# Cross-attention keys: 512-byte pieces and turns on VectorE instead of transposes on TensorE

## The chip, the cores and the metric

The kernel runs on one core of a Trainium2 chip. The metric is the device time of one execution in microseconds (us). Engines are called as in the profile: PE is TensorE, DVE VectorE, ACT ScalarE, POOL GpSimd and SP SyncE.

## What is computed

One inference step of a hybrid decoder layer, for a prompt group (1 x 256 tokens) and a sample group (8 x 4 tokens) that share the weights: a Mamba-2 branch and a gated linear attention branch, merged by gates, then cross-attention into 256 memory tokens, then a convolutional feed-forward network. All data are 32-bit floats. The change is in the cross-attention (4 heads of 512 channels, model width 2048):

```python
def _cross_attend(hn, mem_k, mem_v, w_cq, w_co):
    Bsz, L, _ = hn.shape
    q = (hn @ w_cq).reshape(Bsz, L, CROSS_HEADS, CROSS_HEAD_DIM).astype(jnp.float32)
    s = jnp.einsum('blhd,bmhd->bhlm', q, mem_k.astype(jnp.float32)) * (CROSS_HEAD_DIM ** -0.5)
    pr = jax.nn.softmax(s, axis=-1)
    o = jnp.einsum('bhlm,bmhd->blhd', pr, mem_v.astype(jnp.float32)).astype(hn.dtype)
    return o.reshape(Bsz, L, D_MODEL) @ w_co
```

The prompt attends to keys and values that the kernel has computed and stored earlier; each of the 8 samples has its own keys and values in a cache (8 x 256 x 4 x 512).

## The kernel before, in words

**Tokens and weights.** Activations lie with channels on the 128 partitions and all T = 288 tokens (256 of the prompt, 32 of the samples) along the free dimension. A weight matrix streams through in blocks: `wload` (L108) issues the DMA on SP's queue into one of three `raw` buffers of 512 KB, and `wsplit` (L100) divides a block into a high half, cast by ACT (L103), and a low half, subtracted by DVE (L105); five buffers of each let this run ahead of PE. `proj_w` (L132) then makes three matmuls of 288 columns for every 128 x 128 weight block: high by high, high by low, low by high (L147, L148, L151). It covers 256 output columns at a time in two PSUM banks; `acc_tiles` (L61) alternates between two pairs of banks, so one pair is emptied while the other fills. A "row block" below is 128 input rows against four column blocks, 12 matmuls.

**Order of the work.** `weave` (L172) runs a main generator, the projection of the next head, and after each of its steps the due share of a background generator, the attention of this head. Within that order a scheduler may move instructions of an engine whose dependences allow it, except those held by `keep_in_program_order`. Each engine executes its own queue in order. DMAs issued by POOL stand in POOL's queue, weights in SP's.

**Around the cross-attention.** `gate_b` (L1262) ends the gating, `w_mix_out` is projected (L1303 to L1309) with residuals loaded and stored by POOL in pieces of two tiles, and then the stage begins:

- `q_proj(hd)` (L1359) projects the queries of one head in two passes of 256 columns, each over all 16 row blocks. For each 128 columns DVE scales the sum from PSUM into the one `qs` buffer (L1370), ACT and DVE split it into `qh` and `ql`, and `diag` (L194) spreads the sample columns into `xqm`, which has zeros outside each sample's own columns.
- `attend(hd)` (L1380) takes a key tile of one sample as [128 tokens, 2, 512 channels] (`mem_rows`, L1375, one DMA of 512 KB on POOL's queue, at most four loaded ahead in five buffers), transposes it in eight 128 x 128 blocks through PE (`transpose_half`, L1347, matmuls of L1353 into PSUM), and copies the result out in two halves, one by DVE and one by ACT (L1410), into `kT`. After each four samples `scores` (L1398) multiplies all sample queries with these keys (L1402). The prompt's keys go the same way but are split in two halves (L1421), and the prompt scores are made from them (L1431 to L1433). Softmax (L1338), transposes of the probabilities (L1446, L1455), products with the values of samples (L1464) and prompt (L1474 to L1476), and a fold of the sample rows (L1484) follow. The values of four samples lie in the large buffer `vq` (L1412), those of the others come through the same five buffers as the keys.
- `run(q_proj(0))` stands alone (L1496); then four rounds weave `attend(hd)` with `q_proj(hd + 1)`, in the last round with the first 12 steps of the output projection `w_co` (L1497 to L1499). One such round is called a head's turn below.

Of the kernel before, what the change touches and what calls it, by code (L numbers as in the profile page):

```python
# [20 lines left out]
NB = 8  # L21
# [21 lines left out]
def hybrid_step(ctx: ExitStack, tc: tile.TileContext, I: dict, O: list):  # L43
# [56 lines left out]
    def wsplit(raw):  # L100

        hi = wp.tile(list(raw.shape), F32R, tag="whi", bufs=WB, name="whi")
        S.copy(hi, raw)  # L103
        lo = wp.tile(list(raw.shape), F32R, tag="wlo", bufs=WB, name="wlo")
        V.tensor_tensor(lo, raw, hi, ALU.subtract)  # L105
        return hi, lo
# [1146 lines left out]
    mx = halves(bigr2, "mx")  # L1253
    pc_cm = pool("pc")
# [48 lines left out]
    for j2 in range(KT // 2):  # L1303
# [4 lines left out]
        if j2 + 3 < KT // 2:  # L1308
            load_x(j2 + 3)  # L1309
    rst.append(acc)  # L1310
# [6 lines left out]
    def x4(name):  # L1317
        return px.tile([P, 2, 512], F32, tag="x4", bufs=5, name=name)

    def k4(name):  # L1320
        return px.tile([P, 4, 256], F32, tag="k4", bufs=5, name=name)

# [3 lines left out]
    def q2(name):  # L1326
        return px.tile([P, 2, 256], F32R, tag="q2", bufs=6, name=name)
# [19 lines left out]
    def transpose_half(kv, d2):  # L1347

        a = mm_tile()
        for d in range(2):  # L1350
            for m in range(2):
                dd = 2 * d2 + d
                TR(a[:, d * 256 + m * P:d * 256 + (m + 1) * P], kv[:, m, dd * P:(dd + 1) * P], ident)  # L1353
        return a.rearrange("p (d m) -> p d m", m=256)

# [3 lines left out]
    def q_proj(hd):  # L1359
        qp = []  # L1360
        qps.append(qp)
        for j2 in range(2):
            def cons(j, a, j2=j2):
                if not rc:
                    rc.append(rstd_of())
                if j == 0:
                    qp.append((q2("qh"), q2("ql")))
                d = 2 * j2 + j
                qs = px.tile([P, T], F32, tag="qs", bufs=1, name="qs")
                V.tensor_tensor(qs, a, rc[0], ALU.mult)  # L1370
                split(qp[j2][0][:, j, :], qp[j2][1][:, j, :], qs[:, 0:SEQ])
                diag(xqm[hd % 2][:, d], qs[:, SEQ:T])
            yield from proj(I["w_cq"], 512 * hd + 256 * j2, 256, hn, KT, cons)

    def mem_rows(src, name):  # L1375
        t = x4(name)
        G.dma_start(out=t, in_=src.rearrange("(m p) d -> p m d", p=P))
        return t

    def attend(hd):  # L1380


        xq = xqm[hd % 2]
        loads = [(I["cache_mem_k"][b, :, hd, :], "kc") for b in range(NB)]
        loads += [(o_pmk[0, :, hd, :], "kp"), (o_pmv[0, :, hd, :], "vp")]
        loads += [(I["cache_mem_v"][b, :, hd, :], "vc") for b in range(4, NB)]
        got = []
        vq = big.tile([P, 4, 2, 512], F32, tag="bigf", bufs=1, name="vq")

        def rows():  # L1390
            while loads and len(got) < 4:
                got.append(mem_rows(*loads.pop(0)))
            return got.pop(0)

        ssc = la_tile()
        kT = []

        def scores(q):  # L1398
            for d in range(4):
                for j in (3, 2, 1, 0):  # L1400
                    b = 4 * q + j
                    MM(ssc[NS * j:NS * j + NS, 0:256], xq[:, d, b, :], kT[b][:, d, :], start=(q == 0 and d == 0),  # L1402
                       stop=(q == 1 and d == 3))

        for b in range(NB):
            kc = rows()
            kT.append(k4("kT"))
            for d2 in range(2):
                a = transpose_half(kc, d2)
                (S.copy if d2 else V.tensor_copy)(kT[b][:, 2 * d2:2 * d2 + 2, :], a)  # L1410
            if b < 4:
                G.dma_start(out=vq[:, b], in_=I["cache_mem_v"][b, :, hd, :].rearrange("(m p) d -> p m d", p=P))  # L1412
            yield
            if b == 4:
                scores(0)
                yield
        kp = rows()
        kh, kl = r4("kTh"), r4("kTl")
        for d2 in range(2):
            a = transpose_half(kp, d2)  # L1420
            split(kh[:, 2 * d2:2 * d2 + 2, :], kl[:, 2 * d2:2 * d2 + 2, :], a)  # L1421
        yield
        scores(1)
        yield
        prs = []
        for l in range(2):
# [7 lines left out]
            if l == 0:  # L1434
                pr = k4("prs")[:, 0, :]
# [5 lines left out]
        vp = rows()  # L1441
        vh, vl = v2("vph"), v2("vpl")
        split(vh, vl, vp)
        a = mm_tile()
# [15 lines left out]
        vcs = [vq[:, b] for b in range(4)] + [rows() for _ in range(4)]  # L1460
        for q in (1, 0):
            for m in range(2):
                for j in (3, 2, 1, 0):
                    mm = MM(osa[NS * j:NS * j + NS, :], pms[:, m, 4 * q + j, :], vcs[4 * q + j][:, m, :],  # L1464
                            start=(q == 1 and m == 0), stop=(q == 0 and m == 1))
                    if q == 1 and m == 0 and j == 3:
                        tc.keep_in_program_order(mm)
        yield
        yield
        for d in range(4):  # L1470
# [6 lines left out]
            split(*(x[:, 0:SEQ] for x in co(4 * hd + d)), a[:, 0:SEQ])  # L1477
            yield
        os_ = k4("os").rearrange("p d m -> p (d m)")[:, 0:512]
# [8 lines left out]


# [6 lines left out]
    run(q_proj(0))  # L1496
    for hd in range(4):  # L1497
        main = q_proj(hd + 1) if hd < 3 else chain(steps(wo[0], 6), steps(wo[1], 6))
        weave(main, attend(hd), 16 if hd < 3 else 12, 21)  # L1499
    px_cm.__exit__(None, None, None)  # L1500

# [238 lines left out]
```

## Time and profile before

| What | Value |
|---|---|
| Time, median of 3 runs | 2555.09 us (2553.22 to 2556.65) |
| Profiled execution: span | 2555.0 us |
| PE busy | 2536.1 us, 99% |
| DVE, ACT, POOL busy | 1733.3, 1353.1, 400.0 us |
| Moved by DMA | 521.96 MB, mean 204 GB/s |
| The stage: first query matmul to last fold | about 1416 to 1631 us of the span |

The profile page gives no time of the profiled execution other than its span, from the first to the last instruction. Busy time counts an engine's instructions, overlapped or not, so PE at 99% says that matmuls follow each other closely, not that PE is at its peak. The chain of waits is followed back from the last instruction of a window to whatever released each one; its shares add up to the window. In the table of stages the columns are busy microseconds of PE, PE's weight loads, DVE, ACT and POOL with the number of instructions, then the granted PE clock (1.00 is full), the share of time for which the 16 DMA engines held packets, and the rate in GB/s.

### The profile page before, as it was taken

To read this page: it belongs to the slowest core of one execution; us is meant where nothing else is said; L and a number is where in the kernel's file an instruction comes from. 1 tells how busy PE (TensorE), PEld (TensorE's weight loads), DVE (VectorE), ACT (ScalarE), POOL (GpSimd) and SP (SyncE) were. 2 spreads that over 40 slices of the span, in tenths; PEclk is the share of its full clock that TensorE was granted. 3 is DMA by queue.
4 is the path that set the end of the run, shared out by engine and by line. 5 is a ranking of instruction groups with operands and counts; after the bars stand their busy time and mean duration, and the time that the engine had idled before them with its cause. 6 is when DMAs were issued, how large, how long until landed. Compare 5 with 4: busy or idle time off the path is not lost.

```text
span 2555.0 us, 50480 instructions
## 1 busy us (share of the span) xinstructions
PE 2536.1 (99%) x18966; PEld 2440.0 (95%) x18966; DVE 1733.3 (68%) x3672; ACT 1353.1 (53%) x2712; POOL 400.0 (16%) x741
## 2 busy tenths in 40 slices
PE   9999999999999999999999999999999999999998
PEld 8889999999999999999999989999999999999998
DVE  6656777796767666766556555567777677675765
ACT  7656547645364555444545544456545455454545
POOL 3002234241201000010000122412010101020010
PEclk9999999999999999999999999999999999999999
DMA  8676587776868585777666778755555555555553
GB/s 267 216 223 200 170 243 212 225 208 193 233 194 287 171 259 166 242 234 246 184 207 212 250 260 304 221 172 171 166 175 166 175 166 175 167 171 171 169 172 128
DMA packets 442277, 521.96 MB, mean 204 GB/s; under 512 B 27132, under 2 KB 390492, under 8 KB 441968
## 3 DMA queue, kind: packets, MB, share of 16 engines
q1 hardware_dynamic: 407728, 422.34, 53.7%
q0 software_dynamic: 34272, 96.38, 12.2%
q8 instruction: 149, 2.44, 0.4%
q14 instruction: 96, 0.79, 0.1%
q10 hardware_dynamic: 32, 0.01, 0.0%
HBM read 473.13 MB, written 45.48 MB: 203 GB/s over the span
## 4 chain that ended last, share of the span: by engine, by line
PE 96%; DVE 1%; DMA 1%; issue 0%; ACT 0%; POOL 0%; DVEq 0%; ACTq 0%
PE acc L148 27%; PE acc L147 27%; PE acc L151 26%; PE acc L315 2%; PE acc L316 2%; PE acc L319 2%; PE mm L1353 1%; PE la L1402 1%; PE mm L1147 1%; PE la L1138 1%; PE la L1464 1%; PE mm L1111 1%; DMA raw<-in_w_ssd_out_dram 0%; DMA raw<-in_w_in_dram 0%; PE la L864 0%
## 5 line engine op out<-in xcount | busy, mean ns | idle before, releaser
L105 DVE TENSOR_TENSOR wlo<-raw,whi 128x512 fp32r<-128x512 f32 x1464 | 998.4, 687 | 666.3 <-ACT whi L103 636.1
L103 ACT CAST whi<-raw 128x512 fp32r<-128x512 f32 x1464 | 897.9, 618 | 1023.3 <-PE acc L148 807.9
L147 PE MATMUL acc<-xn,whi 128*128 128x288 f32 (+1 forms) x1936 | 550.7, 300 | 0.0
L148 PE MATMUL acc<-xn,whi 128*128 128x288 f32 (+1 forms) x1936 | 542.4, 296 | 0.0
L151 PE MATMUL acc<-xn,wlo 128*128 128x288 f32 (+1 forms) x1936 | 414.5, 295 | 0.0
L148 PE MATMUL acc<-hf,whi 128*128 128x288 f32 x1408 | 393.3, 295 | 0.0
L147 PE MATMUL acc<-hf,whi 128*128 128x288 f32 x1408 | 389.0, 292 | 0.0
L147 PEld LDWEIGHTS acc<-xn,whi 128*128 128x128 f32 (+1 forms) x1936 | 364.9, 188 | 9.8 <-issue 8.1
L148 PEld LDWEIGHTS acc<-xn,whi 128*128 128x128 f32 (+1 forms) x1936 | 365.1, 189 | 6.8 <-issue 4.8
L151 PEld LDWEIGHTS acc<-xn,wlo 128*128 128x128 f32 (+1 forms) x1936 | 310.8, 188 | 1.3 <-issue 1.1
L151 PE MATMUL acc<-hf,wlo 128*128 128x288 f32 x1408 | 294.4, 290 | 0.0
L148 PEld LDWEIGHTS acc<-hf,whi 128*128 128x128 f32 x1408 | 264.5, 188 | 0.1
L147 PEld LDWEIGHTS acc<-hf,whi 128*128 128x128 f32 x1408 | 264.0, 188 | 0.1
L151 PEld LDWEIGHTS acc<-hf,wlo 128*128 128x128 f32 x1408 | 226.3, 188 | 0.0
L148 PE MATMUL acc<-pr,whi 128*128 128x288 f32 x704 | 196.5, 295 | 0.0
L147 PE MATMUL acc<-pr,whi 128*128 128x288 f32 x704 | 195.0, 293 | 0.0
L151 PE MATMUL acc<-pr,wlo 128*128 128x288 f32 x704 | 147.4, 290 | 0.0
L147 PE MATMUL acc<-un,whi 128*128 128x288 f32 x512 | 145.7, 300 | 1.6 <-DVE ma L955 1.6
L148 PE MATMUL acc<-un,whi 128*128 128x288 f32 x512 | 143.0, 294 | 0.0
L1564 POOL COPY fsp<-fst 128x16 f32<-128x16 f32 x88 | 36.3, 415 | 650.2 <-DVE av L1576 426.5
L148 PEld LDWEIGHTS acc<-pr,whi 128*128 128x128 f32 x704 | 132.3, 188 | 0.0
L147 PEld LDWEIGHTS acc<-pr,whi 128*128 128x128 f32 x704 | 132.0, 188 | 0.0
(508 smaller groups left out, 4347.7 us busy)
## 6 DMA issues: line engine op xcount, KB each, us to landing
raw<-in_w_in_dram SPq DMA_DIRECT2D x240, 512.0 KB
raw<-in_w_up_dram SPq DMA_DIRECT2D x176, 512.0 KB
raw<-in_w_down_dram SPq DMA_DIRECT2D x88, 512.0 KB
raw<-in_w_cv_dram SPq DMA_DIRECT2D x32, 512.0 KB
raw<-in_w_ssd_out_dram SPq DMA_DIRECT2D x32, 512.0 KB
sin<-in_state_gla_dram POOLq DMA_DIRECT2D x32, 512.0 KB, 5.9
out_dram<-sin SPq DMA_DIRECT2D x32, 512.0 KB
raw<-in_w_gla_out_dram SPq DMA_DIRECT2D x32, 512.0 KB
```

The source lines that it names most:

```text
L103: S.copy(hi, raw)
L105: V.tensor_tensor(lo, raw, hi, ALU.subtract)
L147: MM(a, hi[:, k, cs], xh, start=(k0 + s0 + k == 0), stop=False)
L148: MM(a, hi[:, k, cs], xl, start=False, stop=False)
L151: MM(a, lo[:, k, cs], xh, start=False, stop=(k0 + s0 + k == nk - 1))
L315: MM(accs[m], mn_hi[:, kk, ms_], hi[:, 0, :], start=(kk == 0), stop=False)
L316: MM(accs[m], mn_lo[:, kk, ms_], hi[:, 0, :], start=False, stop=False)
L319: MM(accs[m], mn_hi[:, kk, ms_], lo[:, 0, :], start=False, stop=(kk == KT - 1))
L1111: MM(a, kt[:, i, k * P:(k + 1) * P], vt[i], start=True, stop=True)
L1138: MM(osa[NS * j:NS * j + NS, :], qdm[:, k, b, :], sins[b][:, k, :], start=False, stop=(q == 1 and k == 0))
L1147: MM(a, kb[:, k * P:(k + 1) * P], vst, start=True, stop=True)
L1564: G.tensor_copy(sp[:, :, 0:2], st.rearrange("p (b k) -> p b k", k=2))
```

## The change

Keys are loaded so that DVE can finish the transposition. A key tile becomes [128, 1024]: four DMAs, one for each 128 channels i, each writing 32 partitions. Partition 32 i + m holds, for t = 0 to 7, the 128 channels (512 bytes) of token 32 t + m. DVE's transpose works on blocks of 32 x 32; two of them in place (512 columns each) leave on partition 32 i + x channel 128 i + 32 j + x, for j = 0 to 3, of each token. So the channel tile j that a score matmul contracts over consists of four runs of 32 channels, and the query columns are put in the same order when the query weights are split.

For this `q_proj` handles all 512 columns of a head in one pass: its weight loads take rows of 2 KB for two row blocks, all four accumulator banks are held, and the scale factor is computed at the fifth row block. `transpose_half`, the copies to `kT` and the tiles `x4` and `k4` go. A pool `pk`, opened before the gating ends, has ten tiles for keys and values; the first head's keys are loaded one by one during `gate_b`, its prompt keys and values and four samples' values during the projection of `w_mix_out`. Later heads' loads are issued in `attend` at places where their buffers have just been read. The first head's keys are turned beside `q_proj(0)`, four keys of a later head beside the last products of the head before it.

```diff
-    def wsplit(raw):
-
-        hi = wp.tile(list(raw.shape), F32R, tag="whi", bufs=WB, name="whi")
-        S.copy(hi, raw)
-        lo = wp.tile(list(raw.shape), F32R, tag="wlo", bufs=WB, name="wlo")
-        V.tensor_tensor(lo, raw, hi, ALU.subtract)
+    def wsplit(raw, order=None):
+
+        view = (lambda t: t.rearrange(order)) if order else (lambda t: t)
+        shape = list(raw.shape)
+        if order:
+            shape = [shape[0], shape[2], shape[1], shape[3]]
+        hi = wp.tile(shape, F32R, tag="whi", bufs=WB, name="whi")
+        S.copy(view(hi), raw)
+        lo = wp.tile(shape, F32R, tag="wlo", bufs=WB, name="wlo")
+        V.tensor_tensor(view(lo), raw, view(hi), ALU.subtract)
         return hi, lo
...
+    def mem_load(hd, kind, b=0):
+
+        t = pk.tile([P, 1024], F32, tag="k4", bufs=10, name={"k": "kc", "kp": "kp", "vp": "vp", "v": "vc"}[kind])
+        if kind in ("k", "kp"):
+            src = I["cache_mem_k"][b, :, hd, :] if kind == "k" else o_pmk[0, :, hd, :]
+            for i in range(4):
+                tc.keep_in_program_order(G.dma_start(
+                    out=t[32 * i:32 * i + 32].rearrange("p (t x) -> p t x", x=P),
+                    in_=src[:, i * P:(i + 1) * P].rearrange("(t m) x -> m t x", m=32)))
+        else:
...
+    def turn_keys(hd, kind, b=0):
+
+        if (hd, kind, b) not in turned:
+            turned.add((hd, kind, b))
+            t = ktiles[hd, kind, b]
+            for c in range(2):
+                V.transpose(t[:, 512 * c:512 * c + 512], t[:, 512 * c:512 * c + 512])
...
@@ gate_b
         split_from(*mx(t), th, 0.5)
+        if t % 2:
+            mem_load(0, "k", t // 2)
@@ after each pair of w_mix_out
             load_x(j2 + 3)
+        if j2 < 2:
+            mem_load(0, ("kp", "vp")[j2])
+        elif j2 < 6:
+            vq_load(0, j2 - 2)
@@ q_proj
-            yield from proj(I["w_cq"], 512 * hd + 256 * j2, 256, hn, KT, cons)
+        for k0 in range(0, KT, 2):
+            raw = wload(I["w_cq"][k0 * P:(k0 + 2) * P, 512 * hd:512 * hd + 512].rearrange("(k p) n -> p k n", p=P))
+            if k0 == 4:
+                flush()
                 if not rc:
                     rc.append(rstd_of())
...
+            for k in range(2):
+                hi, lo = wsplit(raw[:, k].rearrange("p (i j x) -> p i j x", j=4, x=32), "p j i x -> p i j x")
+                xh, xl = hn(k0 + k)
+                for j in range(4):
+                    a = accs[j][:, 0:T]
+                    wh, wl = (w[:, j].rearrange("p i x -> p (i x)") for w in (hi, lo))
+                    MM(a, wh, xh, start=(k0 + k == 0), stop=False)
+                    MM(a, wh, xl, start=False, stop=False)
+                    MM(a, wl, xh, start=False, stop=(k0 + k == KT - 1))
+                    if k0 + k == KT - 1:
+                        evac(j)
+                yield
@@ attend
-        for b in range(NB):
-            kc = rows()
-            kT.append(k4("kT"))
-            for d2 in range(2):
-                a = transpose_half(kc, d2)
-                (S.copy if d2 else V.tensor_copy)(kT[b][:, 2 * d2:2 * d2 + 2, :], a)
...
+        for b in (4, 5):
+            turn_keys(hd, "k", b)
+            yield
+        scores(0)
+        for b in range(4, NB):
+            mem_load(hd, "v", b)
+        yield
+        for b in (6, 7):
+            turn_keys(hd, "k", b)
+            yield
+        turn_keys(hd, "kp")
...
         scores(1)
+        if more:
+            for b in range(5):
+                mem_load(hd + 1, "k", b)
...
+            mem_load(hd + 1, "k", 5)
...
@@ after the sample values' products
+        if more:
+            for b in (6, 7):
+                mem_load(hd + 1, "k", b)
+            mem_load(hd + 1, "kp")
+            mem_load(hd + 1, "vp")
+            for b in range(4):
+                vq_load(hd + 1, b)
...
@@ in the loop over the prompt's output tiles d
+            if more:
+                turn_keys(hd + 1, "k", d)
...
-    run(q_proj(0))
+    weave(q_proj(0), first_keys(), 16, NB)
```

More of the change, by code (lines that the diff above doesn't have):

```diff
@@ L1380, in attend, with keys @@
+    def keys(t):
+        return t.rearrange("p (t j m) -> p j t m", t=8, j=4)
     def attend(hd):
         xq = xqm[hd % 2]
[L1384 to L1393, printed above, removed]
+        more = hd < 3
@@ L1487, in attend, with first_keys @@
         yield
+    def first_keys():
+        for b in range(NB):
+            turn_keys(0, "k", b)
+            yield
     res = {}
```

75 lines of the change are left out of this document (35 added, 40 removed).

## The prediction

> **What bounds the kernel now.** I read the page of the profile first: its busy line, its DMA queues and the groups of weight halves.
>
> ```profile
> span 2555.0 us, 50480 instructions
> PE 2536.1 (99%) x18966; PEld 2440.0 (95%) x18966; DVE 1733.3 (68%) x3672; ACT 1353.1 (53%) x2712; POOL 400.0 (16%) x741
> ...
> q1 hardware_dynamic: 407728, 422.34, 53.7%
> q0 software_dynamic: 34272, 96.38, 12.2%
> ...
> L105 DVE TENSOR_TENSOR wlo<-raw,whi 128x512 fp32r<-128x512 f32 x1464 | 998.4, 687 | 666.3 <-ACT whi L103 636.1
> L103 ACT CAST whi<-raw 128x512 fp32r<-128x512 f32 x1464 | 897.9, 618 | 1023.3 <-PE acc L148 807.9
> ```
>
> The span is the profiled execution's own time as far as the page tells; it stands 0.09 us under the median of the three runs (2555.09), so sums against it can be read as sums against the median. TensorE (PE) is busy for 99% of it. "Busy" alone proves little, so the next view is the chain of waits inside the stage that the change touches. One turn of a head, from the first key transposes of one head to those of the next, runs from 1492.31 to 1540.97 us. The chain of that window, pieces with start and length:
>
> ```profile
> by line: PE acc L151 18.1%; PE acc L148 17.9%; PE acc L147 17.9%; PE mm L1353 16.2%; PE la L1402 7.9%; PE la L1464 7.3%; PE mm L1432 2.0%; PE mm L1431 2.0%; PE mm L1433 2.0%; PE mm L1474 1.9%; PE mm L1475 1.9%; PE mm L1476 1.9%; PE mm L1484
> 1492.31 0.44 PE mm L1353 x4
> ...
> 1493.28 0.26 PE acc L151 x2
> ...
> 1504.52 1.86 PE la L1402 x32
> ...
> 1528.58 3.57 PE la L1464 x32
> ...
> 1538.49 0.81 PE mm L1484 x8
> ```
>
> Nothing but PE stands in it: no DMA, no DVE, no "issue". L1353, the transposes of the keys through PE, is 16.2% of 48.66 us, 7.9 us per head, and 0.44 us for four says the same: 0.11 us each, 72 per head, 288 in all, 31.6 us. So in this stage PE sets the time, and PE time taken away is time gained, until something else is late. What could be late is read from busy time by stages (PE, PE weight loads, DVE, ACT, POOL; granted clock, DMA share, GB/s): first the projection before the stage, then one turn, the last turn, and two dense stretches of DMA.
>
> ```profile
> 1310.00:1416.00 106.00, 106.00 (x807) 106.00 (x806) 63.95 (x115) 52.88 (x100) 9.40 (x16) 1.00 0.68 222
> 1492.31:1540.97 48.66, 48.66 (x424) 43.27 (x423) 27.33 (x59) 21.74 (x45) 12.78 (x18) 1.00 0.85 280
> 1589.64:1630.00 40.36, 40.17 (x361) 34.92 (x359) 20.70 (x42) 17.99 (x35) 9.50 (x15) 1.00 0.75 255
> ...
> 330.00:340.00 10.00, 10.00 (x78) 10.00 (x78) 8.85 (x20) 4.45 (x8) 7.99 (x13) 1.00 0.98 280
> 1490.00:1500.00 10.00, 10.00 (x82) 10.00 (x82) 5.85 (x13) 4.79 (x10) 2.14 (x3) 1.00 1.03 375
> ```
>
> In a turn DVE works 27.33 and ACT 21.74 of 48.66 us, but the DMA engines are held for 0.85 of it, 41.4 us. That is the resource to watch: a turn that loses 7.9 us of PE has 40.8 us, and the same bytes must come in.
>
> **Part 1: the transposes go.** 288 at 0.11 us are 31.6 us off the chain. The plain matmuls pay for the mixing as well: three lines of 17.9 to 18.1% are 26.2 us per turn, where 192 at 0.131 (106.00 us over 807, the row 1310 to 1416) make 25.2. Some of this 1.0 us goes with the transposes: between 0 and 4 us over four heads; I take 1, because scores and values still break in. PE: -32.6 us.
>
> **Part 2: DVE turns the keys, and the copies go.** The trace has the same operation on the same shape, fed by pieces 32 partitions high, for another state:
>
> ```profile
> L727 POOL DMA_DIRECT2D sqr<-in_state_ssd_dram x128: 649/652/674, 309.5 to 658.9; - x128
> L878 DVE STREAM_TRANSPOSE st<-sqr x32: 668/702/706, 324.5 to 676.9; 128x512 f32<-128x512 f32 x32
> ...
> L1410 DVE COPY kT<-mm 128x512 f32<-128x512 f32 x8 | 5.5, 686 | 2.3 <-PE mm L1353 2.2
> L1410 ACT COPY kT<-mm 128x512 f32<-128x512 f32 x8 | 4.7, 585 | 8.2 <-PE mm L1353 8.2
> L1377 POOL DMA_DIRECT2D kc<-in_cache_mem_k_dram x32 | 22.7, 713 | 97.9 <-PE mm L1353 43.8 <-DVE pms L1449 24.1 <-PE la L1464 17.2
> ...
> DMA to landing us min/median/max: 4.4/6.0/10.3
> ```
>
> The last row is the landing time of the key tiles as they are loaded now.
>
> Nine tiles a head by two turns by 0.702 are 12.6 us more of DVE, less 5.5 of copies: 34.4 us of some 41, 84%. ACT falls by 4.7. PE hides this as long as the halves of the weights (0.69 us of DVE and 0.62 of ACT for every 1.58 us of PE) stay ahead. In place instead of into a second tile has no row; I take the same 0.702. DVE runs in order, so a turn waiting for its key tile holds the next weight halves behind it, and PE waits for those after the five buffers run out. The densest DVE stretch, eleven row blocks from the first turn for the next head to that of its prompt keys, adds two groups of splits:
>
> ```profile
> L189 DVE TENSOR_TENSOR co<-mm,co 128x256 fp32r<-128x256 f32 x4 | 1.7, 423 | 1.3 <-ACT co L188 1.2
> ...
> L189 DVE TENSOR_TENSOR kTl<-mm,kTh 128x512 fp32r<-128x512 f32 x2 | 1.3, 685 | 0.1
> ```
>
> With nine tiles' turns (12.6), eleven weight halves (7.6), four evacuations (4.2, part 4) and these splits (3.0) DVE has 27.4 us; PE has eleven row blocks (17.4), fold, scores (3.7) and value products (5.7% of the chain, 2.8), 24.7 us. A quiet half before it allows some lead. I charge 1 us in each of the three full turns, bounds 0 and 3.
>
> The weight halves of the query projection are written in runs of 32 instead of straight, and the scores read keys in runs of 32; no row shows either. Bounds: nothing; or, if every write took a fifth longer, 0.14 x 16 = 2.2 us of DVE a turn, and if the scores read at half rate, another 3.9 us of PE a turn (7.9% of the chain). A gain has no reason. I take nothing: the element counts are those of the rows quoted, and the keys' turning row already writes blocks at its 0.702.
>
> **Part 3: the loads.** A key tile is four DMAs instead of one. POOL pays 0.65 (pieces with 512 runs) to 0.71 us for each whatever the run length, so 36 key pieces and 9 value tiles are 30 to 32 us of POOL in 41. Nothing else waits for POOL here, and the loads stand where their buffers have just been freed, while before they waited 43.8 us for transposes. By this pace five key tiles need 14 us from the second scores on; the first is turned some 13 us later and lands some 6 after its issue, so 5 to 7 us of slack. On the DMA engines q0 and q1 both move about 309 GB/s of held time (96.38 MB in 12.2%, 422.34 MB in 53.7%, of 2555 us). Nine key tiles, 4.72 MB, hold them 15.3 us a turn. The bound above comes from 330 to 340 us, where pieces of 128 bytes go into 32 partitions beside weights: 280/0.98 = 286 GB/s of held time, against 375/1.03 = 364 at 1490. A ratio of 1.27 on the keys is 4.2 us more: 41.4 to 45.6 us per turn. I take 41.4, the lower end: pieces of 512 bytes lie nearer to whole rows, and the query weights come in 2 KB rows instead of 1 KB (gain unpriced, taken as nothing). PE stayed at 10.00 of 10 under a share of 1.03, so a turn of 41 to 42 us on full queues is possible.
>
> The first head's 14 tiles (7.3 MB) move into the 210 us before. There the share is 0.68; 35 GB/s more makes about 0.8. Each key tile puts 2.8 us of POOL ahead of the residual loads and stores, which are issued three projections ahead. Cost nothing; if raw weights came late, 2 us at most. The issue needs no freed buffer and should start as written.
>
> **Part 4: the query projection in one pass.** All four accumulator banks are in use, so the next head's projection starts on banks that are just being emptied. The evacuation of one bank, from rows of the same turn:
>
> ```profile
> L1370 DVE TENSOR_TENSOR qs<-acc,rstd 128x288 f32<-128x288 f32 x4 | 1.8, 451 | 0.0
> ...
> L189 DVE TENSOR_TENSOR ql<-qs,qh 128x256 fp32r<-128x256 f32 x4 | 1.7, 419 | 0.2 <-ACT qh L188 0.2
> ...
> L194 DVE COPY xqm<-qs 128x32 f32<-128x32 f32 x4 | 0.7, 178 | 0.1
> L188 ACT CAST qh<-qs 128x256 fp32r<-128x256 f32 x4 | 1.6, 404 | 0.4 <-DVE qs L1370 0.4
> ```
>
> With one qs buffer that is 0.45 + 0.40 + 0.42 + 0.18 = 1.45 us per bank in a row, and the fourth bank is read out 3 x 1.45 + 0.45 = 4.8 us after its first. PE has until then three banks of the last row block (1.2), the fold (0.8) and three banks of the next (1.2): 3.2 us. It waits 1.6 us at each of three borders, 4.8 us. Bounds 0, if other matmuls are put in between, and 9.6, if ACT and DVE come late. The move of the scale factor to the fifth row block costs nothing: its matmul was there already.
>
> **Part 5: the last turn** ends in a chain that is not PE:
>
> ```profile
> 1619.16 0.45 issue
> 1619.60 0.35 DVE prp L1345
> 1619.95 0.19 DVE pms L1449 x2
> 1620.21 0.43 DVE vpl L189
> 1620.64 0.61 issue
> 1621.26 0.68 DVE wlo L105
> 1622.05 0.36 DVE prp L1345
> ```
>
> The softmax of the last head already waits about 3.4 us here. With fewer transposes to fill, and key turns in front on DVE, I charge 2 us (0 to 4).
>
> **Sum.** -32.6 + 3 x 1 + 4.8 + 2 = -22.8 us: 2555.0 - 22.8 = 2532 us. With all costs at nothing and all 4 us of mixing gone it is 2519.4; with all at their bounds (9 + 9.6 + 4 + 2, gain 31.6) 2548.
>
> **Rivals.**
> *The DMA becomes the bound, mildly.* The keys take 1.27 times their engine time and a turn is 45.6 us. Three turns gain 3.1 each, the last 5.9: 2555.0 - 15.2 = 2540. For: share 0.85 already. Against: less than that is asked for, and both ends of the stage have room. It lies inside the range.
>
> *DVE takes PE's place.* At 84% with waits on ACT and DMA in order, strided writes at 2.2 us a turn and slower scores (3.9) give back 6.1 of 7.9, and the borders the rest: 2553 to 2556, no difference. Against: the row at 330 us has DVE at 8.85 of 10 and PE at 10.00.
>
> *The key pieces hold the DMA engines twice as long, and the change is slower.* A piece writes to 32 partitions only. If that halves their rate, keys hold 30.6 us a turn and the whole turn 56.7. Over three turns 170 us must fit, and the slack of the first key turn, some 7 us, is there once; then DVE stands at a turn with weights behind it. (170 - 7)/3 = 54.3 us per turn, 5.6 more than now, three times 17, less 5.9 in the last: 2566. It decides from the point where the three turns lose more than the 5.9 us of the last, at about 1.75 times. Against: the row at 330, where pieces of this form fill 32 partitions, and 1.27 is all that it shows.
>
> [...]
>
> **How the numbers follow.** A measurement of this kernel can tell 0.2%, 5.1 us, from no change. Forecast with its bounds: 0.58. The mild DMA bound: 0.12. DVE in PE's place: 0.09. Slower by the pieces: 0.21, of which 0.01 stays within 0.2%. Faster is 0.58 + 0.12 + 0.02 of the DVE case = 0.72; same 0.07 + 0.01 = 0.08; slower 0.20. The range runs from 2521, leaving 0.02 below, to 2562, leaving 0.18 of the slower case above.
>
> **What would show it.** The key transposes gone from the chain, and a turn of 41 to 43 us with PE still at its full length: right. Gaps of PE between the last and first row block of two heads of 1 to 2 us: part 4 right. DVE turns waiting for key tiles, weight halves waiting behind them and a DMA share of 1.0: the rivals. If the scores' line grows past 0.06 us a matmul, or weight halves past 0.7 us, part 2 was wrong. A stage before it longer than now would break the early loads.

## The result, and the profile after

| | Median (range) | Profiled span |
|---|---|---|
| Before, beside it on the same chip | 2553.94 us (2550.80 to 2558.14, 20 runs) | 2555.0 us |
| After | 2557.19 us (2550.01 to 2562.42, 20 runs) | 2556.5 us |

The ratio is 1.001, 95% interval 1.0003 to 1.0017: no difference beyond the 0.2% that a measurement here can tell. The forecast said 22.8 us less. The time lies inside the range, the forecast itself was wrong. From here on the "stage" runs from the first weight load of the query projection to the first of the feed-forward network.

The page of after, the rows that answer to those of before:

```profile
span 2556.5 us, 50096 instructions
PE 2514.2 (98%) x18678; PEld 2412.1 (94%) x18678; DVE 1749.1 (68%) x3712; ACT 1332.6 (52%) x2680; POOL 459.4 (18%) x849
...
q1 hardware_dynamic: 399536, 422.34, 54.6%
q0 software_dynamic: 36000, 96.38, 12.8%
...
L109 DVE TENSOR_TENSOR wlo<-raw,whi 128x512 fp32r<-128x512 f32 x1464 | 994.8, 687 | 656.0 <-ACT whi L107 645.4
```

PE is busy 22 us less, and the span does not shrink: the work went and came back as waiting. The same bytes hold the DMA engines longer, q0 by 0.6% of the span and q1, on which the weights come, by 0.9%. Where the time goes is read from the first starts of two lines, the query projection's and the feed-forward network's. The line ahead of them is the last fold of the gated linear attention, which runs ahead of all changed code. Before:

```profile
L1161 PE MATMUL mm<-fold,os x32: 190/276/276, 834.0 to 1175.2; 128*128 128x32 f32 x32
...
L147 PEld LDWEIGHTS acc<-hn,whi x256: 186/188/192, 1415.9 to 1585.6; 128*128 128x128 f32 x128
...
L147 PEld LDWEIGHTS acc<-hf,whi x1408: 187/188/190, 1713.0 to 2437.1; 128*128 128x128 f32 x176
```

and after:

```profile
L1165 PE MATMUL mm<-fold,os x32: 190/276/276, 834.1 to 1175.3; 128*128 128x32 f32 x32
...
L1417 PEld LDWEIGHTS acc<-hn,whi x256: 186/188/219, 1424.8 to 1567.5; 128*128 128x128 f32 x128
...
L151 PEld LDWEIGHTS acc<-hf,whi x1408: 187/188/189, 1714.4 to 2438.6; 128*128 128x128 f32 x176
```

The stage lasted 297.1 us and lasts 289.6 us, 7.5 less; but it begins 8.9 us later, and the fold shows that none of this lateness is older than the change: its last matmul starts at 1175.2 and at 1175.3 us. The loss ahead of the stage lies at one place, the gating, where the first head's keys are now loaded. The chain of 1185 to 1240 us holds nothing but PE before:

```profile
by line: PE acc L151 33.9%; PE acc L148 33.4%; PE acc L147 32.8%
```

The same chain of after, and then that of 1425 to 1640 us, reduced to their DMA waits:

```profile
by line: DMA raw<-in_w_in_dram 39.8%; DMA raw<-in_w_gla_out_dram 25.3%; PE acc L151 8.1%; PE acc L152 8.0%; PE acc L155 7.6%; ACT whi L107 4.6%; DVE wlo L109 3.9%; issue 2.7%; ACTq L107 0.2%; DVE mb L959 0.1%
...
1191.53 13.91 DMA raw<-in_w_gla_out_dram
...
1207.50 10.57 DMA raw<-in_w_in_dram
...
1220.15 11.33 DMA raw<-in_w_in_dram
```

```profile
1464.65 13.18 DMA kc<-in_cache_mem_k_dram
1507.06 14.49 DMA raw<-in_w_cq_dram
1556.49 12.24 DMA raw<-in_w_co_dram
1589.92 6.00 DMA kc<-in_cache_mem_k_dram
1599.51 6.51 DMA vq<-in_cache_mem_v_dram
```

Both hold what the chains of before lacked (from 1425 to 1640 us too, no DMA stands in that of before): transfers that PE waits for, weights above all. The busy time by stages (columns as before) shows the same, first for before, then for after:

```profile
1195.00:1235.00 40.00, 40.00 (x306) 40.00 (x305) 24.65 (x45) 17.50 (x30) 2.46 (x5) 1.00 0.71 220
1490.00:1600.00 110.00, 110.00 (x948) 99.22 (x948) 61.95 (x134) 49.44 (x100) 28.40 (x40) 1.00 0.86 291
...
1600.00:1630.00 30.00, 29.81 (x277) 24.56 (x275) 15.38 (x34) 13.12 (x27) 6.65 (x11) 1.00 0.66 215
```

```profile
1195.00:1235.00 40.00, 33.17 (x236) 31.27 (x236) 15.64 (x31) 10.06 (x18) 18.70 (x32) 1.00 1.02 268
1490.00:1600.00 110.00, 104.55 (x853) 92.25 (x852) 75.53 (x165) 43.34 (x90) 60.63 (x101) 0.98 1.03 293
1600.00:1630.00 30.00, 20.81 (x171) 14.85 (x170) 15.31 (x34) 7.37 (x17) 5.37 (x9) 0.89 0.54 199
```

From 1490 to 1600 us the engines are held for 1.03 of the time and move no more than 293 GB/s, against 291 at a share of 0.86 before. PE stands idle 5.5 us there, 9.2 us from 1600 to 1630 us, in the last turn, and 6.8 us in the gating. The granted clock is 0.89 in the last turn, while in the gating it stays at 1.00 in spite of the gaps. A turn, which was to take 41.4 to 45.6 us, takes 48.9 from fold to fold, about as long as before (48.66):

```profile
1492.40:1541.30 48.90, 45.93 (x380) 39.12 (x379) 33.51 (x78) 19.77 (x43) 26.97 (x45) 1.00 1.03 300
```

The rate followed what was under way:

```profile
1490.00:1500.00 10.00, 10.00 (x84) 8.80 (x82) 9.38 (x24) 3.31 (x8) 5.79 (x11) 1.00 1.04 255
1500.00:1510.00 10.00, 10.00 (x99) 7.82 (x98) 4.59 (x8) 2.81 (x5) 6.04 (x10) 1.00 1.02 359
```

255 GB/s is a stretch of key pieces beside weights, 359 one in which value tiles are issued, at nearly equal share.

### The profile page after: what moved, and what is told of

Same layout as the page of the kernel before. It is cut to its first block, busy times and chain, and to the rows that moved or that the text cites. A ratio compares the mean times of both kernels' runs of the same rounds, so it can differ in the third digit from the quotient of the medians.

```text
span 2556.5 us, 50096 instructions
## 1 busy us (share of the span) xinstructions
PE 2514.2 (98%) x18678; PEld 2412.1 (94%) x18678; DVE 1749.1 (68%) x3712; ACT 1332.6 (52%) x2680; POOL 459.4 (18%) x849
## 4 chain that ended last, share of the span: by engine, by line
PE 92%; DMA 4%; DVE 1%; POOL 1%; ACT 1%; issue 0%; SPq 0%; DVEq 0%; ACTq 0%; POOLq 0%
PE acc L152 25%; PE acc L151 25%; PE acc L155 25%; PE acc L319 2%; PE acc L320 2%; PE acc L323 2%; DMA raw<-in_w_in_dram 1%; PE acc L1417 1%; PE acc L1418 1%; PE acc L1419 1%; DMA kc<-in_cache_mem_k_dram 1%; PE mm L1151 1%; PE la L1142 1%; DMA raw<-in_w_cq_dram 1%; DMA raw<-in_w_gla_out_dram 1%; PE mm L1115 1%
```

## The experiments

Theory at first: the key pieces, written to 32 partitions, hold the DMA engines too long, and this costs the gain. Rivals: the turns on DVE; the one-pass projection; the early loads by themselves. In each table the ratio is to before on the same chip; "start" and "stage" are those of the profiled execution, as above (before: 1415.9 and 297.1; after: 1424.8 and 289.6). "Ahead" is the time from the last fold of the gated linear attention to that start (before: 240.7; after: 249.5). It is the better measure of the early loads: that fold, ahead of all edits, starts between 1169.0 us (g_widenoturn) and 1176.8 us (i_half), a scatter that starts and spans take along. "Middle" and "last" are the two middle turns and the last, from the start of one head's fold of the sample rows to that of another's (before: 97.3 and 42.4; after: 102.5 and 35.3).

**Pieces and turns.** Four edits of after, with the rest as it is:

```diff
 a_wide512: four pieces of 512-byte rows, but into all 128 partitions
-  out=t[32 * i:32 * i + 32].rearrange("p (t x) -> p t x", x=P),
-  in_=src[:, i * P:(i + 1) * P].rearrange("(t m) x -> m t x", m=32)
+  out=t[:, 256 * i:256 * i + 256].rearrange("p (m x) -> p m x", x=P),
+  in_=src[:, i * P:(i + 1) * P].rearrange("(m p) x -> p m x", p=P)
 b_narrow2k: into 32 partitions, but in rows of 2 KB
+  out=t[32 * i:32 * i + 32].rearrange("p (m d) -> p m d", m=2),
+  in_=src[64 * i:64 * i + 64, :].rearrange("(m p) d -> p m d", p=32)
 d_noturn: the key pieces as in after, without V.transpose
-  V.transpose(t[:, 512 * c:512 * c + 512], t[:, 512 * c:512 * c + 512])
 g_widenoturn: a_wide512 and d_noturn together
```

In all four the scores are made from keys in another order than the queries', so only their times are read.

> The changed kernel, but each of the four DMAs of a key tile writes runs of 512 bytes into all 128 partitions instead of 32 (tokens and channels land in other places, so scores are of a wrong arrangement; bytes, run length, number of DMAs and all other work are the same). Theory 1, the 32 partitions: the keys' packets fall from some 254 ns to 160 to 200, the DMA share in the stage falls below 1.0 and the time to 2533 to 2543 us. Theory 2, the run length of 512 bytes: packets and time stay, 2553 to 2560. Theory 3, DVE: no change either, 2553 to 2560.

> The other half of the pair: each of the four DMAs writes 32 partitions, as in the changed kernel, but in whole rows of 2 KB (again a wrong arrangement of tokens and channels). Theory 1, the 32 partitions: packets stay near 250 ns and the time at 2552 to 2560 us. Theory 2, the run length: packets fall to 160 to 200 ns and the time to 2533 to 2543. Theory 3, DVE: 2553 to 2560.

> The changed kernel without the DVE turns (keys are used unturned, so this part of the computation is left out): 12 us of DVE less per head. If the DMA engines bound the stage (theories 1 and 2): within 3 us of the changed kernel, 2553 to 2559 us. If DVE had taken the place of PE (theory 3): 2546 us or less.

> Both suspects taken away from the changed kernel: keys in runs of 512 bytes into all 128 partitions, as in a_wide512, and no DVE turns, as in d_noturn (keys are used unturned and in a wrong arrangement). If the slow pieces and the turns on DVE together ate the gain, this comes near the forecast: 2530 to 2536 us. If a third cost is there (the projection's borders, the last head's softmax chain, the clock), 2540 or more.

| Kernel | Median (range), us | Ratio (95%) | Span | Start | Ahead | Stage | Middle | Last |
|---|---|---|---|---|---|---|---|---|
| a_wide512 | 2545.93 (2542.61 to 2551.07) | 0.997 (0.9957 to 0.9982) | 2542.8 | 1414.6 | 242.5 | 286.0 | 95.7 | 38.3 |
| b_narrow2k | 2562.64 (2555.19 to 2563.57) | 1.0029 (1.0016 to 1.0043) | 2558.5 | 1423.1 | 252.0 | 293.2 | 102.3 | 40.0 |
| d_noturn | 2549.25 (2544.22 to 2556.71) | 0.9981 (0.9972 to 0.9991) | 2546.5 | 1420.4 | 249.0 | 284.0 | 102.8 | 30.3 |
| g_widenoturn | 2534.48 (2534.05 to 2539.26) | 0.9926 (0.9908 to 0.9945) | 2532.3 | 1413.6 | 244.6 | 276.5 | 94.7 | 29.8 |

The times of a_wide512 and d_noturn came out between those that their theories gave; each cause has a part. By the ratios the pieces cost some 10 us, the turns 7, both together 21; from the fold to the end of the stage (ahead and stage together: after 539.1 us, before 537.8) it is 10.6, 6.1 and 18.0. So they nearly add up. With both away most of the forecast gain is there: 18.9 us by the ratio (14 to 23), 16.7 from the fold on, of 22.8. The places differ: with pieces in place of wide ones the two middle turns take 7 to 8 us more, and 4 to 7 more are lost ahead of the stage; with the turns on DVE the last turn takes 5 to 9 us more, the middle ones nearly the same. It is the 32 partitions and not the 512-byte runs: b_narrow2k, with rows of 2 KB, is no faster than after (ratios 1.0029 and 1.001). In the chain of a_wide512 from 1425 to 1640 us no DMA stands any more. What the pieces do to the engines stands on its page:

```profile
span 2542.8 us, 50097 instructions
...
q1 hardware_dynamic: 399536, 422.34, 54.2%
q0 software_dynamic: 36000, 96.38, 12.1%
```

Shares times spans: q0 307.7 us of all 16 engines against 327.2 in after, q1 1378 against 1396. The 36 key tiles, 18.9 MB, hold the engines about 61 us at the 309 GB/s of the prediction. Their own queue takes 20 us longer, 1.3 times; the weights that run beside them pay another 18 us, so the price is some 1.6 times, an estimate as the 61 us are. The trace has the packets of the first head's keys one by one, 1024 of 4 KB between 1185 and 1245 us: 254 ns each on average in after, 178 in a_wide512, 1.4 times. What the turns do is read from g_widenoturn beside after's rows; its last turn runs from 1575 to 1605 us:

```profile
1490.00:1600.00 110.00, 105.67 (x887) 93.75 (x884) 58.77 (x133) 44.90 (x95) 67.52 (x94) 0.97 0.87 307
...
1554.00:1564.00 10.00, 10.00 (x79) 10.00 (x79) 9.90 (x30) 7.14 (x16) 9.08 (x14) 1.00 0.78 254
1584.00:1594.00 10.00, 6.34 (x65) 4.82 (x64) 6.19 (x18) 4.19 (x10) 1.01 (x2) 0.95 1.02 394
```

DVE falls from 75.5 to 58.8 of 110 us. The turns themselves kept their duration. Where they bind in the stage of after, its waits (us, times, longest) and its chain show:

```profile
L1285 DVE STREAM_TRANSPOSE kc<-kc x64: 662/672/712, 1240.4 to 1609.0; 128x512 f32<-128x512 f32 x64
```

```profile
PE la L1437 <- DVE kc L1285: 4.8, 1, 4.8
```

```profile
1606.63 3.05 DVE kc L1285 x5
```

Scores waited 4.8 us for a turn of a key tile, once, and the chain of the last head's turn holds five key turns in a row. The two kernels without key turns have the shorter last turn. For weight halves that queue behind turns on DVE, the way that the prediction had in mind, PE waited some 1 us at most in the stage.

**The one-pass projection alone**, put into before with straight columns:

```diff
-  yield from proj(I["w_cq"], 512 * hd + 256 * j2, 256, hn, KT, cons)
+  accs = acc_tiles(2) + acc_tiles(2)      # then the loop of q_proj of the change
```

> The kernel before with one part of the change alone: the query projection of a head in one pass over all four accumulator banks, in natural channel order; keys still go through PE. The prediction charged 1.6 us at each of three borders: 4.8 us slower than before, some 2559 us. If the scheduler puts other matmuls in between, 2554 to 2556. If this part ate the gain, 2565 or more.

2555.43 us (2552.63 to 2559.24), ratio 1.0001 (0.9991 to 1.001). The borders cost nothing here; other matmuls stand in them. The transposes are among these still, but g_widenoturn has none and its PE is busy without a gap from 1416 to 1584 us, with the borders at about 1439, 1480, 1515 and 1555 us in it.

**The early loads.** In after the 32 key DMAs of the first head depend on nothing, so POOL issues them one behind another, from 1195 to 1227 us, instead of one tile per pair of gating tiles. c_paced and f_paced2 put a small POOL copy of `th` ahead of each load, so that it waits for its pair; f_paced2 also has a scratch tile of 512 bytes in place of 16 and keeps the first head's turns in program order. q_late and t_late_pinned move the loads into the loop of `w_mix_out`, the second with the first head's turns kept in program order as in f_paced2.

```diff
 c_paced, f_paced2
+  tc.keep_in_program_order(G.tensor_copy(pace, th[:, 0:4]))
   mem_load(0, "k", t // 2)
 q_late, t_late_pinned
-  if t % 2:
-      mem_load(0, "k", t // 2)
...
+  mem_load(0, "k", j2)      # for each pair of tiles of w_mix_out
   if j2 < 2:
       mem_load(0, ("kp", "vp")[j2])
```

> The changed kernel, but each of the first head's eight key loads stands behind a small POOL copy from the gate tile of its place, so they come one by one, some 13 us apart, instead of in a burst. Theory of the burst: the 9 us by which the query projection starts later are back, 2545 to 2550 us. If the same bytes cost the same wherever they come, or the lateness has another source: 2553 to 2558.

> The changed kernel with the first head's key loads paced by a POOL copy of the gate tile, as in c_paced, but the copy's scratch tile takes 512 bytes instead of 16, so that the key tiles keep their place in the row, and the first head's key turns stay behind the work that stands ahead of them on DVE. Theory of the burst: the query projection starts near 1416 us of the span, not 1425, and the time is 2546 to 2550 us. If c_paced was slow because pacing itself starves the stage: 2570 or more.

> The changed kernel, but the first head's key tiles are loaded one per pair of tiles of the projection of w_mix_out, behind that pair's residual store, and not during the gating. If the burst of loads without a dependence is what makes the first query matmul 9 us late, it comes at 1414 to 1417 us, and the time is 2546 to 2550. Rival (the pieces cost the same wherever they go in, as an earlier paced run suggested, which got back the gating but lost 7 us beside w_mix_out): first query matmul at 1420 us or later, time 2552 to 2557.

> As q_late, with the first head's turns held at their place beside its query projection, so that no turn waits for a key tile during the projection of w_mix_out. If the burst of loads without a dependence makes the 9 us, the first query matmul comes at 1414 to 1418 us, the stage lasts 289 us as in the changed kernel, and the time is 2546 to 2551, the best of the correct versions. If the pieces cost the same wherever they go in, the first query matmul comes at 1420 us or later and the time is 2552 to 2558.

| Kernel | Median (range), us | Ratio (95%) | Start | Ahead | Stage |
|---|---|---|---|---|---|
| c_paced | 2578.15 (2573.95 to 2579.10) | 1.0089 (1.0073 to 1.0106) | 1426.2 | 253.7 | 309.2 |
| f_paced2 | 2555.75 (2551.80 to 2564.84) | 1.0006 (0.9995 to 1.0018) | 1420.0 | 248.7 | 288.8 |
| q_late | 2564.72 (2554.86 to 2571.18) | 1.0037 (1.0024 to 1.0049) | 1430.3 | 257.6 | 297.0 |
| t_late_pinned | 2564.62 (2559.41 to 2569.44) | 1.0043 (1.0029 to 1.0057) | 1423.1 | 252.9 | 294.9 |

None gained against after or before, and none separates the burst from what came with it. In c_paced the key tiles moved by 16 bytes as well (below). In all four, kept in program order or not, turns ran ahead into the projection of `w_mix_out`, and DVE stood 23 to 29 us before key tiles between 1195 and 1425 us, which it does not do there in after; PE waited 4 to 7 us there for weight halves. The gating got its time back and the projection behind it lost it. t_late_pinned, busy time beside `w_mix_out` and pieces of its chain there, then DVE's waits for key tiles in its whole run (us, times):

```profile
1312.00:1420.00 108.00, 100.14 (x737) 96.97 (x736) 59.80 (x112) 46.29 (x91) 29.03 (x49) 1.00 0.80 236
```

```profile
1344.87 1.64 POOL kc L1268 x3
1346.62 7.95 DMA kc<-in_cache_mem_k_dram
...
1355.68 0.42 DVE hx L1334
...
1361.33 10.62 DMA raw<-in_w_mix_out_dram
```

```profile
  DVE kc L1285: 33.5, 10
```

PE loses 7.9 us, at a mean share of only 0.80: the chain goes over weight blocks, and over a key tile whose turn holds up the residual sum `hx` on DVE. So with pieces the stage starts 8 to 12 us later than before wherever the first head's keys go in (ahead, without q_late and c_paced); how much of it the burst makes stays open.

**What is left without pieces and turns**: m_allpe_straight loads every key tile by one DMA in whole rows and transposes it on PE, with straight query columns, copied back in place; early loads, ten buffers and the one-pass projection stay.

```diff
-  for i in range(4):
-      tc.keep_in_program_order(G.dma_start(out=t[32 * i:32 * i + 32]...
+  tc.keep_in_program_order(G.dma_start(out=t.rearrange("p (m d) -> p m d", m=2), in_=src.rearrange("(m p) d -> p m d", p=P)))
...
+  TR(a[:, j * 256 + m * P:j * 256 + (m + 1) * P], kv[:, m, (2 * j2 + j) * P:(2 * j2 + j + 1) * P], ident)
```

> Every key tile whole, transposed by PE in contiguous blocks, copied back in place by DVE and ACT; query columns in straight order; early loads, ten buffers and one-pass projection as in the changed kernel. Theory (pieces and turns carry the whole loss, the rest is free): 2552 to 2557, the time of before, with weight halves back at 0.68 us, and the first query matmul at 1416 us or a little earlier. Rival (the new places of the loads or the early loads cost by themselves): 2562 or more, with DMA waits in the chain of the stage.

2567.15 us (2565.54 to 2569.79), ratio 1.0053 (1.0041 to 1.0065), start 1423.5, ahead 249.9, stage 299.9. The rival held in the time, though its DMA waits stand in the gating and not in the chain of the stage: without pieces the early loads still cost 9.2 us. Busy time in the gating and the issue of the keys there, m_allpe_straight:

```profile
1195.00:1235.00 40.00, 35.91 (x249) 35.42 (x249) 19.85 (x38) 13.62 (x25) 3.66 (x6) 0.91 0.87 291
```

```profile
L1277 POOL DMA_DIRECT2D kc<-in_cache_mem_k_dram x8 | 5.6, 708 | 4.5 <-DMA mar<-mg_d 3.1 <-DMA mg_d<-mq 0.8 <-issue 0.6
```

and a_wide512, which lost only 1.8 us ahead of the stage (g_widenoturn 3.9), the same group:

```profile
L1268 POOL DMA_DIRECT2D kc<-in_cache_mem_k_dram x32 | 23.0, 721 | 5.7 <-DMA mar<-mg_d 2.1 <-DMA mg_d<-mq 1.5 <-ACT whi L107 0.8
```

The same 4.2 MB are asked for in 5.6 us of POOL in the one, in 23 us in the other. That POOL's four issues per tile pace them, so that weights get through, fits these kernels but is argued, not shown; with 32 partitions the same four issues per tile lost 8.8 us ahead of the stage (after). The stage of m_allpe_straight is 2.8 us longer than that of before, which was not followed further.

**Where in a partition the pieces land.** The slowness of c_paced led to this. A scratch tile is put ahead of the key and value tiles, which moves them and what is allocated behind them:

```diff
 h_shift16 (4 floats), l_shift64 (16), p_shift1024 (256)
+  pad = pk.tile([P, 4], F32, name="pad")
+  G.memset(pad, 0.0)
```

> The changed kernel with nothing but a tile of 16 bytes per partition allocated ahead of the key and value tiles, so that each of them starts 16 bytes further in its partition. If c_paced was slow because of this shift (its key packets took 335 to 348 ns instead of about 255): 2570 to 2580 us, with packets above 300 ns. If the shift does nothing: 2555 to 2560.

> The changed kernel, with a scratch tile of 64 bytes per partition ahead of the key tiles, where an earlier run had 16 bytes and took 22 us longer. If only the place within 64 bytes counts, the time is that of the changed kernel, 2555 to 2559. If any move of the key tiles costs (or the scratch tile itself does), 2575 to 2580 again.

> The changed kernel with 1024 bytes of scratch per partition ahead of the key tiles. If alignment of the landing place counts, the time is that of the changed kernel, 2554 to 2560. If the scratch tile itself, or any move, costs: 2574 to 2580, as with 16 and 64 bytes.

| Scratch | Median (range), us | Ratio (95%) |
|---|---|---|
| 16 bytes | 2578.86 (2569.69 to 2583.58) | 1.0089 (1.0063 to 1.0115) |
| 64 bytes | 2576.59 (2570.16 to 2577.43) | 1.0081 (1.0068 to 1.0093) |
| 1024 bytes | 2556.08 (2549.42 to 2561.22) | 1.0009 (1.0 to 1.0018) |

It is the place where the tiles land, not the scratch tile itself: 16 and 64 bytes cost 20 and 18 us against after by the ratios, 1024 nothing, nor do the 512 of f_paced2 (ratio 1.0006). The page of h_shift16 and its stage:

```profile
q0 software_dynamic: 36000, 96.38, 13.4%
```

```profile
1490.00:1600.00 110.00, 98.07 (x763) 87.98 (x762) 69.47 (x153) 37.64 (x80) 55.60 (x92) 0.94 1.04 266
```

q0 is held 345 us instead of 327, and the rate is 266 GB/s instead of 293. What makes these two places slow, and what offsets between 64 and 512 bytes would cost, was not shown.

**Mixtures meant to beat both kernels.** Four of nine tiles as pieces with turns, five whole and through PE. In i_half every fourth channel makes a channel tile, so that both paths agree; j_allpe is its control with no pieces. r_half32_late keeps the order of runs of 32 and builds each block from four matmuls of 32 columns, with late loads.

```diff
 i_half, j_allpe
+  TR(a[:, ...], kv[:, m].rearrange("p (c j) -> p j c", j=4)[:, 2 * j2 + j], ident)
+  v = t[:, 512 * c:512 * c + 512].rearrange("p (t x j) -> p t j x", x=32, j=4)
 r_half32_late
+  MM(a[32 * i:32 * i + 32, ...], kv[:, m, c0:c0 + 32], ident, start=True, stop=True)      # c0 = P * i + 32 * (2 * j2 + j)
```

> A mixture meant to beat both kernels. Of each head's nine key tiles the first four samples' still come in 32-partition pieces and are turned by DVE; the other four and the prompt's come as whole rows into 128 partitions and go through PE in eight transposes each, copied back into the same tile. So that both paths give the same channel order, channel tile j is every fourth channel. Theory (the pieces hold the DMA engines 1.6 times as long, and the turns cost some 7 us): 16 of 36 tiles leave PE, 128 transposes at 0.11 us, -14 us; the surplus of held DMA time in a turn falls by five ninths, from some 10 to some 4.5 us, so PE at 45 and DMA at 45 to 46 us a turn balance, against 48.7 before: 2541 to 2547. Rival (any use of the pieces beside full queues spoils it, or PE reads keys with a stride of 16 bytes slower): 2555 or more; in that case the scores' line shows more than 0.06 us a matmul.

> The same with no pieces at all: every key tile as whole rows, transposed by PE, copied back in place by DVE and ACT; early loads, ten buffers, and one-pass query projection as in the changed kernel. It tells what is left of the change without its pieces and turns. If everything else in the change is free, PE has all its transposes again and the time is that of before, 2553 to 2557. If the early loads or the new places of loads help, it is below 2551; if they cost something by themselves, above 2560.

> Late loads as in the run beside it, and of each head's nine tiles only the first four as pieces with turns; five whole, transposed by PE. The channel order is that of the changed kernel: each 128 x 128 block is made by four matmuls of 32 stationary columns against the identity, to four groups of partitions. If such four cost what one transpose cost (0.11 us), PE saves 14 us, a turn's DMA surplus is four ninths, and the time is 2540 to 2546: better than both kernels. If each costs 0.06 us as a score matmul does, the five tiles take 9.6 us a turn in place of 4.4, and the time is 2560 or more.

i_half 2569.44 us (2565.60 to 2573.24), ratio 1.0058 (1.0044 to 1.0072); j_allpe 2569.16 (2565.66 to 2572.45), 1.0058 (1.0044 to 1.0072); r_half32_late 2583.59 (2582.67 to 2588.30), 1.0119 (1.0104 to 1.0135). Two relatives, i_half with the first head all on PE and r_half32_late with early loads, came to 2572.72 and 2579.81. All missed. Late loads did not help r_half32_late either: its stage starts 252.7 us behind the fold, that of its relative with early loads 245.1, where 6 to 9 us the other way had been expected. Groups of i_half in the stage:

```profile
L109 DVE TENSOR_TENSOR wlo<-raw,whi 128x512 fp32r<-128x512 f32 x79 | 79.8, 1030 | 45.3 <-ACT whi L107 44.4 <-PE la L1461 0.9
...
L1305 DVE STREAM_TRANSPOSE kc<-kc 128x512 f32<-128x512 f32 x24 | 26.1, 1141 | 3.9 <-DMA kc<-in_cache_mem_k_dram 3.9
```

Weight halves whose neighbours are written 512 bytes apart and turns in steps of 16 bytes are 1.6 and 1.7 times as long as the 687 and 672 ns of after (the 79 halves include some of `w_co` in straight order; their median is 1.10 us). The halves are no large price: j_allpe has them too, and m_allpe_straight, with straight ones, is no more than 0.05% faster. And in r_half32_late:

```profile
L1297 PE MATMUL mm<-ident,kc 128*32 128x128 f32 x1024 | 34.1, 275 | 0.0
```

Sixteen tiles take 34.1 us, 2.1 us each, where eight transposes took 0.9; that was the dearer case of its expectation. So none of the versions with the whole computation beats both kernels; whether one exists is open.

## Why the prediction was wrong, step by step

- **What bounds the kernel**: right. PE set the time, and 0.85 of DMA share was named as the resource to watch.
- **Part 1, -32.6 us**: the work went: 288 matmuls fewer (18966 to 18678), 21.9 us of PE busy time. Why not the whole 31.6 was not settled.
- **Part 3 is the step that failed**: "A ratio of 1.27 on the keys is 4.2 us more: 41.4 to 45.6 us per turn. I take 41.4". It charged the pieces nothing. They cost 7 to 8 us over the two middle turns, near the upper end of 4.2 us each, and 4 to 7 us ahead of the stage, where Part 3 had at most 2. Against a_wide512, the keys' own queue does take 1.3 times; but the weights beside them take as much again, some 1.6 in all, and with the same runs into 128 partitions the kernel is some 10 us faster than after. The row at 330 us was read as bytes over held time of a mixture, which hides how the price is shared: of the 2.8 MB that moved there only some 0.6 were pieces into 32 partitions (nine issues of 64 KB), so that 1.27 for the whole would be over 2 on them alone, by an estimate. Its lower end was then preferred because 512 is nearer to whole rows than 128; run length is not what counted here (b_narrow2k, 2562.64 us with rows of 2 KB).
- **Part 3, early loads, "Cost nothing; if raw weights came late, 2 us at most"**: wrong; ahead of the stage after loses 8.8 us. The mean share of 0.68 was read, but the loads came in the gating, at 0.71 before and 1.02 after: loads without a dependence were issued one behind another within 32 us, and the chain waits 10.6 to 13.9 us for each of three weight blocks. What a slower pace alone would have saved was not shown.
- **Part 2, 3 us for the turns**: taken out, they give 6 to 7 us, but in the last turn; the two middle ones lose 1 us at most. The duration, 0.67 to 0.70 us, was right, and the weight halves kept theirs (687 ns).
- **Part 4, 4.8 us at the borders**: wrong in the other direction; 0 within 0.1% either way (e_onepass), and no gap at a border of g_widenoturn, which has no transposes to fill it.
- **Part 5, 2 us in the last turn**: too small; the turns alone cost 5 to 9 us there. PE stands idle 9.2 of 30 us there in after, where the chain waits 6.51 us for a value tile. Even in g_widenoturn PE lacks 5.0 of the 29.9 us from 1576.01 to 1605.91, at a clock of 0.89, and there the chain goes over DVE and ACT.
- **Rivals**: "The key pieces hold the DMA engines twice as long" had the mechanism and the sign of its warning signs: a share of 1.03, waits for keys and weights in the chain. Its size, some 1.6 and not 2, lies below the 1.75 from which it alone would have been slower. No run shows the half of the rate that it assumed for 32 partitions; shown are packets 1.4 times as long, 254 ns against 178. "DVE takes PE's place" is the second part of the answer, with 6 to 7 us.
- The span with both causes away, 2532.3 us, is the forecast to 0.3 us. That is luck: 6.2 us of it arose ahead of the changed code, and the gain is 17 to 19 us. Without the 3 us for turns, which that kernel doesn't have, and the 4.8 for borders, which cost nothing, the sum would gain 30.6; 3.9 us ahead of the stage and 5.0 in the last turn, for 2 forecast, are part of what is missing.

## What to carry to other kernels

Price a DMA by the partitions that it writes and by what it does to the queue beside it, not by bytes and run length alone: the same 512-byte runs cost some 10 us less here into 128 partitions than into 32 (a_wide512), and rows of 2 KB into 32 cost no less (b_narrow2k). When a stage already holds the engines for 0.85 of its time, take the dear end of the range: the turn that was to take 41.4 to 45.6 us took 48.9. Loads that depend on nothing were issued as a burst here, 32 in 32 us, and their cost fell on the stream of weights that ran at that moment, with waits of 10.6 to 13.9 us for each of three blocks, whatever the mean share of 0.68 in a longer stretch. Moving such loads later was no remedy by itself (q_late 1.0037, t_late_pinned 1.0043): the turns that wait for them moved along, and DVE, which starts its instructions in the order of the program (all 3712 of after), stood 23 to 29 us before key tiles. Before spans of single executions are compared, look whether they run alike up to the first changed instruction. Before work is moved off the bounding engine, count what the two resources behind it have left once it is faster.

## What the runs showed of the hardware

- In after, a stretch with pieces into 32 partitions beside weights (1490 to 1500 us) moved 255 GB/s at a DMA share of 1.04, the next one, with value tiles into 128 partitions, 359 at 1.02.
- The price of such pieces fell about as much on the other queue as on their own: 18 and 20 us of held time (after against a_wide512).
- Moving their landing place by 16 or 64 bytes cost 20 and 18 us more (h_shift16, l_shift64), by 512 or 1024 bytes nothing (f_paced2, p_shift1024).
- Weight halves whose neighbours are written 512 bytes apart took 1.10 us in the median (i_half) instead of 0.69 (after).
- The granted PE clock was 0.89 in the last turn of after, where PE stood idle 9.2 of 30 us; in the gating, with 6.8 idle of 40, it stayed at 1.00.
